# Forgetting attention in a two-layer decoder step: query, sample and memory steps tied by order edges to places between the heads, and the samples' scores taken one PSUM bank at a time

## The chip, the cores and the metric

The program runs on one core of one Trainium2 chip, in one launch. The metric is the device time of one execution in microseconds (us), lower is better. The engines are named as in the profile: PE (TensorE, matrix products), PEld (its weight loads), DVE (VectorE), ACT (ScalarE), POOL (GpSimd) and SP (SyncE, whose queue issues most of the DMA transfers). PE writes only to PSUM, whose eight banks of 128 x 512 float32 hold all products until DVE or ACT has read them.

## What is computed

One inference step of a trunk of two layers for a prompt of 512 tokens and eight samples of four new tokens each, width 1024. Layer 0 has a state-space and a sliding-window branch; layer 1, which the change touches, has forgetting attention. Every layer then has cross-attention into 256 memory tokens and a SwiGLU feed-forward part.

```python
def fox_attend(q, k, v, cum, q_off):
    '''Queries sit at key indices q_off..q_off+Tq-1; logit[t,s] += cum[t]-cum[s].'''
    ...
    bias = cq[..., :, None] - c[..., None, :]
    mask = jnp.arange(tk)[None, :] <= (q_off + jnp.arange(tq))[:, None]
    return gqa_attend(q, k, v, mask=mask, bias=bias)

def mem_kv(mem, g, wk, wv):
    b, m, _ = mem.shape
    mn = rms_norm(mem, g)
    return ((mn @ wk).reshape(b, m, XA_HEADS, XA_HEAD_DIM),
            (mn @ wv).reshape(b, m, XA_HEADS, XA_HEAD_DIM))
```

There are 16 query heads and 4 key heads of width 64. The prompt attends to itself in blocks of 128 queries; each sample attends to 1024 cached tokens, which lie in eight pages named by a table, and to its own four.

## The kernel before

All matrix products that need float32 precision are split: a weight piece of 128 x 1024 is loaded into one of two raw buffers (`wpiece`, L158), its high part made by ACT (L162) and its low part by DVE (L163) in one of three pairs of buffers, and three matmuls take the place of one (`acc3`, L138). The next load waits on SP's queue until a raw buffer has been split.

The attention of layer 1 is written in `odd`. Its prompt part has 64 **heads**: for each half m of the query heads (2), each block c of 128 queries (4) and each of eight query heads, `fox_prompt` computes scores (two matmuls of width W = 128(c+1) into a bank), then DVE subtracts the mask, negates and takes the row minimum (L1160, tensor_tensor_reduce), ACT takes the exponential with its sum (L1161), DVE the reciprocal (L1162), and POOL scales (L1163). Two heads later (`FOX_AHEAD`) the probabilities are transposed by PE (`tr`, L141), copied to `PT` by DVE or ACT (L1143), and after the eighth head of a block multiplied with the values (`pv`) and copied out (L1150). Heads 1 to 16 have W = 128 and 256, heads 17 to 32 have W = 384 and 512, heads 33 to 64 repeat this.

Between the heads three generators are advanced by a table of head numbers, `FOX_PLAN`:
- **q**: the second half of the query projection, eight steps of 24 matmuls (`linear_steps`), evacuated by DVE (L456);
- **s**: the samples, four groups G of two samples, in `fox_sample`: scores of 1024 cached tokens into two banks of the tag `sc` (a forget term from `S`, then the keys `fox_k`), scores of the new tokens (`sn`), maximum and exponential (L1272 to L1279), transposes (copied by ACT, L1288), the product with the values `fox_v`, its scaling into `sO` (ACT, L1296) and a transposition into q. The keys and values of group G + 1 are loaded through SP (L1237), 16 transfers each;
- **m**: the memory tokens' normalised operands (`mem_begin`: eight splits on ACT, L251, and on DVE, L252), then their keys and values (four steps of 24 and four of 12 wide matmuls).

After the heads the outcome is split (`oh`, `ol`) and multiplied with the output weights `wo_d`; the first products need only the first 256 tokens.

The order on each engine isn't the order in which the program is written. The program's order gives priorities; a scheduler that plays the program through with modelled times puts on each engine what is ready, and the result is the fixed order of that engine's queue. An order edge (`after`) holds one instruction behind another one in that order, without a semaphore. PSUM tiles are drawn by tag, and a tag's number of buffers caps how many of it live at once: `bufs = {"tr": 3, "sc": 2, "tp": 2, "pv": 1}`. Heads below 33 draw their score bank from `sc` alone, later heads from `['sc', 'sc', 'tr']` in turn.

Of the kernel before, what the change touches and what calls it, by code (L numbers as in the profile page):

```python
# [14 lines left out]
AF = mybir.ActivationFunctionType  # L15
ALU = mybir.AluOpType
# [3 lines left out]
P = 128  # L20
# [86 lines left out]
class Net:  # L107
    def __init__(self, nc, tc, ctx, I, O):
        self.nc, self.tc, self.ctx, self.I, self.O = nc, tc, ctx, I, O
        self.n = self.turn = 0  # L110
        self.hold = self.whold = self.last = None
# [25 lines left out]
    def mm(self, out, lhsT, rhs, start, stop):  # L137
        self.nc.tensor.matmul(out, lhsT, rhs, start=start, stop=stop)  # L138

    def tr(self, out, in_, k=P):  # L140
        self.nc.tensor.transpose(out, in_, self.ident[0:k, 0:k])  # L141
# [846 lines left out]
    def odd(self, st, nxt, fill):  # L988
        nc, tc, I, O = self.nc, self.tc, self.I, self.O
        with ExitStack() as es:  # L990
# [53 lines left out]
            with tc.tile_pool(name="fox", bufs=1) as fx:  # L1044
# [13 lines left out]
                self.banks = ['sc']  # L1058
# [4 lines left out]
                for m in range(2):  # L1063
                    for c in range(4):
# [22 lines left out]
    def fox_keys(self, kT, ncum):  # L1087
# [21 lines left out]
        self.zero(mask[:, 0:384])  # L1109
        self.after(nc.gpsimd.tensor_copy(mask[:, 384:512], self.cst[:, C_SWA + 128:C_SWA + 256]), self.last)  # L1110
# [15 lines left out]
    def fox_prompt(self, q, K2, V, m, c, ahead):  # L1126
# [4 lines left out]
        Q = self.fox_queries(q, m, tok)  # L1131
# [19 lines left out]
        for r in range(2):  # L1151
            for i in range(4):
                sc = self.bank([P, 512])
                for z in range(2):
                    self.mm(sc[:, 0:W], Q[z][:, r, i], K2[z][:, m, r, 0:W], z == 0, z == 1)
# [64 lines left out]
    def fox_sample(self, q, kTs, Qb, ncs, V, lf, fx, S, sel):  # L1220
# [25 lines left out]
        self.sample_q(q, Qb)  # L1246
        for G in range(4):
            sc = [self.psum("sc", [P, 4, 128]), self.psum("sc", [P, 4, 128])]
            sn = self.psum("tp", [P, 32])
            for u in range(2):  # L1250
                self.mm(sc[u].rearrange("p a b -> p (a b)"), sel[:, 128 * (G % 2):128 * (G % 2) + 128], S[:, G // 2, 512 * u:512 * u + 512], True, False)
                for b2 in range(2):
                    for m in range(2):
                        a = 64 * b2 + 32 * m
                        lq = Qb[:, 2 * G + b2, m].rearrange("p r i t -> p (r i t)")
                        self.mm(sc[u][a:a + 32], lq, keys[G, b2][:, 4 * u:4 * u + 4, 128 * m:128 * m + 128], False, True)
# [7 lines left out]
            wk = self.prt[:, 2560:4736]  # L1264
            pr = wk[:, 0:1056]
            gate = nc.vector.tensor_tensor(pr[:, 1024:1056], sn, c[:, C_MN + 32 * G:C_MN + 32 * G + 32], ALU.add)
            if G < 3:
                load(keys, G + 1, "fox_k")
            yield
            mx, nm, den, d1, rec = self.ty(3), self.ty(1), self.ty(3), self.ty(1), self.ty(1)  # L1270
            for u in range(2):
                nc.vector.tensor_reduce(mx[:, u:u + 1], sc[u].rearrange("p a b -> p (a b)"), AX.X, ALU.max)  # L1272
            nc.vector.tensor_reduce(mx[:, 2:3], pr[:, 1024:1056], AX.X, ALU.max)
            nc.vector.tensor_reduce(nm, mx, AX.X, ALU.max, negate=True)
            for u in range(2):
# [21 lines left out]
            self.sample_o(q, Osb, G, 1)  # L1297
            if G < 3:
                load(vals, G + 1, "fox_v")
            yield  # L1300


    def mem_begin(self, l):
# [12 lines left out]
        for k in range(KD):  # L1316
            g = self.par[:, G_MEM + 8 * l + k:G_MEM + 8 * l + k + 1]
            self.split(mh, ml, raw[:, k], k, 0, 256, g)
            if first:
                self.square_acc(acc, raw[:, k], k, 256)  # L1320
        if first:
            self.rstd(acc, self.mcol, self.mb, [(0, 0, 128), (1, 128, 128)])
# [381 lines left out]
    def run(self):  # L1704
# [5 lines left out]
        def memory(l):  # L1710
# [3 lines left out]
            m = self.mem_begin(l)  # L1714
# [129 lines left out]
```

## Time and profile before

| what | value |
|---|---|
| median of 3 runs | 1694.12 us (1693.13 to 1695.23) |
| profiled execution | 1698.67 us, span 1696.9 us |
| busy share of the span | PE 97%, PEld 89%, DVE 70%, ACT 46%, POOL 19% |
| chain that ended last | PE 91%, DVE 3%, POOL 2%, ACT 1%, DMA 1% |
| the heads of layer 1 | about 1005 to 1189 us of the span |

An engine's busy time counts its instructions from start to end. Matmuls are pipelined, so a busy PE need not be at its peak. An idle time is put down to the instruction whose semaphore ended it.

### The profile page before, as it was taken

The page shows a single profiled execution, that of the slowest core. Times are in us where ns is not written, and L with a number is a line of the kernel's source. Part 1 is how long each engine was busy: PE and PEld are TensorE (multiplying, and loading weights), DVE is VectorE, ACT ScalarE, POOL GpSimd, SP SyncE. Part 2 cuts the span into 40 slices and gives each one's busy share as a digit, 9 for nine tenths or more (in the row PEclk, how much of TensorE's full clock was granted, in tenths as well). Part 3 has the DMA queues.
Part 4 walks back from the last instruction along what each step waited for, and adds up shares of the span by engine and source line. Part 5 has one row for each costly group of instructions (what it writes and reads, how often), then busy time and mean ns, then how long its engine had stood idle before and what let it go on. Part 6 is the DMA issues. An engine that isn't in the chain of part 4 may idle for free.

```text
span 1696.9 us, 32362 instructions
## 1 busy us (share of the span) xinstructions
PE 1645.9 (97%) x12720; PEld 1518.7 (89%) x12720; DVE 1184.0 (70%) x2296; ACT 778.3 (46%) x1603; POOL 328.3 (19%) x510
## 2 busy tenths in 40 slices
PE   6999999998999999999999998998999999999997
PEld 6988899886997999999999996655988999999997
DVE  7667678867766887677766567654567877777663
ACT  5255445344444544444445355544545444444444
POOL 5022312657422310000001203111223100000002
PEclk9999999999999999999999999999999999999999
DMA  5211424126533233232323334554551233223222
GB/s 185 63 55 39 145 82 132 51 91 237 207 100 125 81 113 102 89 103 88 106 75 107 127 116 125 160 174 149 181 178 59 75 113 100 94 100 106 75 68 86
DMA packets 71221, 189.27 MB, mean 112 GB/s; under 512 B 7612, under 2 KB 34012, under 8 KB 63452
## 3 DMA queue, kind: packets, MB, share of 16 engines
q1 hardware_dynamic: 69388, 184.84, 32.9%
q8 instruction: 100, 1.64, 0.4%
q10 hardware_dynamic: 1600, 1.83, 0.4%
q0 software_dynamic: 80, 0.52, 0.1%
q14 instruction: 53, 0.43, 0.1%
HBM read 172.22 MB, written 14.95 MB: 110 GB/s over the span
## 4 chain that ended last, share of the span: by engine, by line
PE 91%; DVE 3%; POOL 2%; ACT 1%; issue 1%; DMA 1%; SPq 0%; DVEq 0%; POOLq 0%; ACTq 0%
PE ps L138 66%; PE ps L1563 22%; PE ps L141 3%; POOL room L425 1%; DMA room<-wo_d 0%; POOL sq L421 0%; DVE split_t L1544 0%; ACT prt L1161 0%; DVE prt L1160 0%; DVE xs L879 0%; ACT split_t L162 0%; DMA mem<-mem 0%; DVE meml L252 0%; DVE x L1730 0%; DMA x<-x 0%
## 5 line engine op out<-in xcount | busy, mean ns | idle before, releaser
L138 PE MATMUL ps<-xh,split_t 128*128 128x288 f32 (+1 forms) x2304 | 463.8, 294 | 13.8 <-ACT split_t L162 11.8
L138 PEld LDWEIGHTS ps<-xh,split_t 128*128 128x128 f32 x2304 | 371.1, 190 | 19.8 <-ACT split_t L162 12.8
L1563 PE MATMUL ps<-xf,split_t 128*128 128x272 f32 x2592 | 348.9, 289 | 3.1 <-DVE split_t L1544 2.1
L138 PE MATMUL ps<-xl,split_t 128*128 128x256 f32 (+1 forms) x1152 | 339.1, 295 | 1.2 <-DVE xl L252 1.0
L1563 PEld LDWEIGHTS ps<-xf,split_t 128*128 128x128 f32 x2592 | 335.0, 188 | 4.4 <-DVE split_t L1544 3.0
L261 POOL TENSOR_TENSOR room<-room,sq 128x256 f32<-128x256 f32 (+1 forms) x96 | 86.4, 904 | 773.4 <-ACT sq L260 771.7
L138 PEld LDWEIGHTS ps<-xl,split_t 128*128 128x128 f32 x1152 | 218.9, 190 | 6.9 <-issue 4.3
L138 PE MATMUL ps<-hh,fs 128*128 128x256 f32 (+1 forms) x1024 | 206.3, 288 | 0.0
L162 ACT CAST split_t<-room 128x1024 fp32r<-128x1024 f32 (+1 forms) x128 | 130.3, 1019 | 156.5 <-PE ps L138 112.3
L163 DVE TENSOR_TENSOR split_t<-room,split_t 128x1024 fp32r<-128x1024 f32 (+1 forms) x128 | 157.0, 1229 | 31.5 <-ACT split_t L162 31.0
L138 PEld LDWEIGHTS ps<-hh,fs 128*128 128x128 f32 x1024 | 164.9, 188 | 0.4 <-ACT fs L1607 0.4
L1544 DVE TENSOR_TENSOR split_t<-fr,split_t 128x1024 fp32r<-128x1024 f32 x108 | 131.7, 1221 | 35.3 <-ACT split_t L1543 35.0
L1543 ACT CAST split_t<-fr 128x1024 fp32r<-128x1024 f32 x108 | 113.4, 1052 | 89.6 <-PE ps L1563 53.4
L138 PE MATMUL ps<-hl,fs 128*128 128x256 f32 (+1 forms) x512 | 147.3, 288 | 0.0
L138 PE MATMUL ps<-oh,split_t 128*128 128x288 f32 (+1 forms) x512 | 105.7, 298 | 1.3 <-ACT oh L246 1.2
L138 PEld LDWEIGHTS ps<-hl,fs 128*128 128x128 f32 x512 | 96.4, 188 | 0.0
L138 PEld LDWEIGHTS ps<-oh,split_t 128*128 128x128 f32 x512 | 83.2, 192 | 8.3 <-issue 5.0
L138 PE MATMUL ps<-ol,split_t 128*128 128x288 f32 (+1 forms) x256 | 77.1, 301 | 0.3 <-DVE ol L249 0.2
L1607 ACT CAST fs<-room 128x512 fp32r<-128x512 f32 x64 | 39.4, 618 | 82.6 <-PE ps L138 68.3
L252 DVE SCALAR_TENSOR_TENSOR xl<-x,room,xh 128x256 fp32r<-128x256 f32 (+1 forms) x96 | 69.6, 755 | 5.6 <-ACT xh L251 5.6
L138 PE MATMUL ps<-hh,split_t 128*128 128x256 f32 (+1 forms) x384 | 73.4, 288 | 0.0
L1620 DVE TENSOR_TENSOR x<-x,ps 128x256 f32<-128x256 f32 (+1 forms) x128 | 54.4, 433 | 26.9 <-PE ps L138 26.7
(423 smaller groups left out, 3091.2 us busy)
## 6 DMA issues: line engine op xcount, KB each, us to landing
fr<-wfi SPq DMA_DIRECT2D x36, 1024.0 KB
room<-wfo SPq DMA_DIRECT2D x64, 256.0 KB
room<-wo_e SPq DMA_DIRECT2D x16, 512.0 KB
xk<-mem_k SPq DMA_DIRECT2D x8, 1024.0 KB
xv<-mem_v SPq DMA_DIRECT2D x8, 1024.0 KB
room<-wfi SPq DMA_DIRECT2D x16, 512.0 KB
fox_k<-fox_k SPq DMA_DIRECT2D x64, 128.0 KB
fox_v<-fox_v SPq DMA_DIRECT2D x64, 128.0 KB
```

What stands on the lines that cost most here:

```text
L138: self.nc.tensor.matmul(out, lhsT, rhs, start=start, stop=stop)
L141: self.nc.tensor.transpose(out, in_, self.ident[0:k, 0:k])
L162: nc.scalar.copy(hi[:, 0:n], raw[:, 0:n])
L163: nc.vector.tensor_tensor(lo[:, 0:n], raw[:, 0:n], hi[:, 0:n].bitcast(F32), ALU.subtract)
L252: return nc.vector.scalar_tensor_tensor(ll, src, g, hh.bitcast(F32), ALU.mult, ALU.subtract)
L261: nc.gpsimd.tensor_tensor(acc, acc, sq[:, 0:N], ALU.add)
L425: nc.gpsimd.tensor_tensor(acc, acc, sq, ALU.add)
L1543: nc.scalar.copy(hi, t)
L1544: nc.vector.tensor_tensor(lo, t, hi.bitcast(F32), ALU.subtract)
L1563: self.nc.tensor.matmul(ps, w[a][:, k], x[:, b, k], start=start and k == 0 and i == 0, stop=k == 3 and i == 2, skip_group_check=True)
L1607: nc.scalar.copy(hi, raw)
L1620: nc.vector.tensor_tensor(x, x, ps, ALU.add)
```

## The change

Five things change, all in layer 1's attention:
- the table `FOX_PLAN`, and a call `ready`, which builds the next block's queries four heads before the block begins;
- **order edges**: the first PE instruction of each generator step is held behind the score matmul of the head after which the step stands (`behind`, `placed`);
- **banks**: `tr` 4 and `sc` 3, and all heads draw from `['sc', 'sc', 'tr']`;
- **samples**: the scores come in two halves, each in one bank and a step of its own; DVE copies each half out with its row minimum (the fused operation of the heads, with zeros for the mask), so the bank is free before the exponential, which is then one ACT instruction over 1056 columns in place of three; the last transposition becomes a step of its own. A group has five steps in place of four, of which 17 stand in the table and the rest of the last group follows all heads;
- `mem_begin` is cut into four steps.

```diff
-for _a, _heads in (("q", range(4, 33, 4)), ("s", [33,34,36,38,40,41,43,45,47,49,51,53,55,57,59,61]), ("m", range(34, 64, 4))):
+for _a, _heads in (("q", (2, 4, 7, 10, 13, 16, 20, 24)), ("s", (25, 26, 28, 31, 33, 34, 36, 40, 41, 42, 44, 47, 49, 50, 52, 56, 58)), ("m", (19, 21, 23, 25, 35, 37, 39, 46, 54, 60))):
...
-        bufs = {"tr": 3, "sc": 2, "tp": 2, "pv": 1}[tag]
+        bufs = {"tr": 4, "sc": 3, "tp": 2, "pv": 1}[tag]
...
-        self.nc.tensor.matmul(out, lhsT, rhs, start=start, stop=stop)
+        return self.placed(self.nc.tensor.matmul(out, lhsT, rhs, start=start, stop=stop))
...
+    def placed(self, i):
+        if self.behind is not None:
+            self.behind, d = None, self.behind
+            self.after(i, d)
+        return i
...
-                self.banks = ['sc']
+                self.banks = ['sc', 'sc', 'tr']
...
-                        for _ in self.fox_prompt(q, K2, V, m, c, ahead):
-                            heads += 1
-                            self.banks = ['sc'] if heads < 33 else ['sc', 'sc', 'tr']
-                            for a in FOX_PLAN.get(heads, ""):
-                                next(gens[a], None)
-                self.fox_turn(ahead, 0)
+                blocks = [(m, c) for m in range(2) for c in range(4)]
+                ready = lambda m, c: self.fox_queries(q, m, slice(128 * c, 128 * c + 128))
+                Q = ready(*blocks[0])
+                for j, (m, c) in enumerate(blocks):
+                    for _ in self.fox_prompt(Q, q, K2, V, m, c, ahead):
+                        heads += 1
+                        if heads % 8 == 4 and j < 7:
+                            nq = ready(*blocks[j + 1])
+                        for a in FOX_PLAN.get(heads, ""):
+                            self.behind = self.scored
+                            next(gens[a], None)
+                        self.behind = None
+                    Q = nq
+                for _ in range(FOX_AHEAD):
+                    next(gens["m"], None)
+                    self.fox_turn(ahead, len(ahead) - 1)
...
+                nc.vector.tensor_tensor_reduce(pr[:, 512 * u:512 * u + 512], sf, self.zeros.to_broadcast([P, 512]), -1.0, 1e30, ALU.add, ALU.min, mx[:, u:u + 1])
+                if u == 0:
+                    yield
...
-            for u in range(2):
-                nc.scalar.activation(pr[:, 512 * u:512 * u + 512], sc[u].rearrange("p a b -> p (a b)"), AF.Exp, bias=nm, accum_out=den[:, u:u + 1])
-            nc.scalar.activation(pr[:, 1024:1056], pr[:, 1024:1056], AF.Exp, bias=nm, accum_out=den[:, 2:3])
-            nc.vector.tensor_reduce(d1, den, AX.X, ALU.add)
-            nc.vector.reciprocal(rec, d1)
+            nc.vector.tensor_reduce(nm, mx, AX.X, ALU.min)
+            nc.scalar.activation(pr, pr, AF.Exp, bias=nm, scale=-1.0, accum_out=den)
+            nc.vector.reciprocal(rec, den)
...
+            elif k % 2:
+                yield
```

The table shows little of where instructions now stand. Outside the attention of layer 1 the order of every engine is the same. Three places inside it follow (rows of equal instructions are merged with their count; the number behind a name tells tiles apart).

On PE around heads 18 to 20 (W = 384), before: `kh` and `kl` rows are a head's two score matmuls, `room,prt` rows transposes, a `PT` row the values' product, and the first row is the last matmul of the eighth query step.

```order
L138 MATMUL ps_12024<-xh_10309,split_t 128x288
L141 MATMUL ps_11580<-room,prt 128x128 x2
L141 MATMUL ps_11594<-room,prt 128x128 x2
L141 MATMUL ps_11608<-room,prt 128x128 x2
L138 MATMUL ps_11692<-kh_10826,qst 128x384
L138 MATMUL ps_11692<-kl_10827,qst 128x384
L141 MATMUL ps_11622<-room,prt 128x128 x2
```

The same place in the change:

```order
L138 MATMUL ps_11713<-kh_10826,qst 128x384
L138 MATMUL ps_11713<-kl_10827,qst 128x384
L138 MATMUL ps_11727<-kh_10826,qst 128x384
L138 MATMUL ps_11727<-kl_10827,qst 128x384
L141 MATMUL ps_11612<-room,prt 128x128 x2
L141 MATMUL ps_11655<-room,prt 128x128 x2
L138 MATMUL ps_11778<-kh_10826,qst 128x384
L138 MATMUL ps_11778<-kl_10827,qst 128x384
L138 MATMUL ps_11747<-kh_10826,qst 128x384
L138 MATMUL ps_11747<-kl_10827,qst 128x384
L138 MATMUL ps_11803<-xh_10099,split_t 128x256
L138 MATMUL ps_11803<-xl_10100,split_t 128x256
```

Before, all eight query steps are over by head 18. Now six stand before head 17, the seventh (`ps_11803`) behind head 20 and the eighth behind head 24; the scores of two heads stand together.

On ACT around the eight splits of the memory operands (`memh`), before; 128x512 and 128x128 rows of `prt` are exponentials of heads with that width:

```order
L1161 ACTIVATE prt,ty_12011<-prt,ty_12010 128x512
L1143 COPY PT_11901<-ps_12017 128x2x128
L1143 COPY PT_11902<-ps_12017 128x2x128
L1161 ACTIVATE prt,ty_12060<-prt,ty_12059 128x128
L251 ACTIVATE memh_12313<-mem_12308,room 128x256 x8
L1161 ACTIVATE prt,ty_12269<-prt,ty_12268 128x128
```

The same place in the change:

```order
L1176 ACTIVATE prt,ty_11889<-prt,ty_11888 128x384
L1158 COPY PT_11757<-ps_11895 128x2x128
L1158 COPY PT_11758<-ps_11895 128x128
L1137 CAST qst<-q_1101_11132 64x512
L1176 ACTIVATE prt,ty_11931<-prt,ty_11930 128x512
L258 ACTIVATE memh_11772<-mem_11767,room 128x256 x8
L1158 COPY PT_11757<-ps_11965 128x2x128
L1158 COPY PT_11758<-ps_11965 128x128
L1176 ACTIVATE prt,ty_11959<-prt,ty_11958 128x512
```

The splits move from behind head 33 to behind the first exponential of the heads 25 to 32; they are still eight in a row.

On SP where the output weights `wo_d` are loaded, before; `fox_v_13379` is the second half of the last group's values:

```order
L1237 DMA fox_v_13379<-fox_v 128x256
L1237 ISA
L1237 DMA fox_v_13379<-fox_v 128x256
L158 DMA room<-wo_d 128x1024 x2
L1351 DMA o_p_mem_v<-mkv_12306 128x1024
L1233 ISA x2
L158 DMA room<-wo_d 128x1024
```

The same place in the change, where two `wo_d` loads have gone out ahead of the first of the 16 value loads:

```order
L1252 DMA fox_v_13270<-fox_v 128x256
L165 DMA room<-wo_d 128x1024
L1252 ISA
L1252 DMA fox_v_13270<-fox_v 128x256
L1252 ISA
L1252 DMA fox_v_13270<-fox_v 128x256
L1252 ISA
L1252 DMA fox_v_13270<-fox_v 128x256
L165 DMA room<-wo_d 128x1024
L1368 DMA o_p_mem_v<-mkv_11765 128x1024
```

Before, two `wo_d` loads stand ahead of the last group's 16 key and 16 value loads and the third behind them all; now two stand between keys and values and the third ahead of the last three value loads. The last group's softmax, values' product and output stand among the first `wo_d` products on PE.

## Rows read from the trace of the kernel before

**Rows 1.** Stretches: busy time of each engine, PE clock, DMA share, GB/s

```profile
1005.00:1035.00 30.00, 30.00 (x232) 28.05 (x231) 23.98 (x78) 16.44 (x45) 6.14 (x14) 1.00 0.57 172
1035.00:1064.00 29.00, 24.22 (x120) 14.40 (x119) 21.89 (x71) 17.21 (x48) 10.43 (x21) 1.00 0.26 81
1064.00:1100.00 36.00, 34.85 (x307) 24.26 (x307) 25.30 (x84) 21.37 (x59) 6.05 (x13) 1.00 0.54 157
1100.00:1150.00 50.00, 48.09 (x348) 28.37 (x348) 26.71 (x94) 22.70 (x64) 8.30 (x16) 0.97 0.57 169
1150.00:1189.00 39.00, 33.14 (x246) 22.50 (x244) 18.47 (x57) 17.77 (x50) 5.36 (x8) 0.96 0.51 160
```

**Rows 2.** Waits in 1005 to 1035: us in total, times, longest

```profile
DVE ty L1162 <- ACT prt L1161: 3.2, 6, 0.7
```

**Rows 3.** Waits in 1035 to 1064

```profile
PEld ps L138 <- DVE ty L1160: 6.8, 9, 0.9
...
PE ps L138 <- DVE ty L1160: 3.5, 7, 0.7
DVE ty L1162 <- ACT prt L1161: 3.5, 6, 1.0
```

**Rows 4.** Timeline of DVE: start, duration, what, idle before and its releaser

```profile
1054.00 0.17 DVE L1162 RECIPROCAL ty<-ty 128x1 f32<-128x1 f32 x1 [0.98 <-ACT prt L1161]
1054.08 0.67 DVE L1160 CUSTOM_DVE_ANT_0 prt<-ps,prt 128x512 f32<-128x512 f32 x1
...
1055.73 0.67 DVE L1160 CUSTOM_DVE_ANT_0 prt<-ps,prt 128x512 f32<-128x512 f32 x1
```

**Rows 5.** Groups of DVE in 1003 to 1190: count, busy us, mean ns, idle before

```profile
L163 DVE TENSOR_TENSOR split_t<-room,split_t 128x1024 fp32r<-128x1024 f32 x13 | 16.0, 1234 | 5.3 <-ACT split_t L162 5.3
...
L1160 DVE CUSTOM_DVE_ANT_0 prt<-ps,prt 128x512 f32<-128x512 f32 x16 | 10.8, 673 | 0.0
...
L1272 DVE TENSOR_REDUCE ty<-ps 128x1 f32<-128x512 f32 x8 | 5.5, 689 | 2.8 <-PE ps L138 2.7
...
L252 DVE SCALAR_TENSOR_TENSOR meml<-mem,room,memh 128x256 fp32r<-128x256 f32 x8 | 3.4, 466 | 0.0
...
L456 DVE SCALAR_TENSOR_TENSOR q<-ps,room 128x288 f32<-128x288 f32 x5 | 2.3, 452 | 1.7 <-PE ps L138 1.6
```

**Rows 6.** Groups of ACT in 1003 to 1190

```profile
L1161 ACT ACTIVATE prt<-prt,ty 128x512 f32<-128x512 f32 x16 | 11.6, 724 | 7.4 <-DVE ty L1160 7.4
...
L1276 ACT ACTIVATE prt<-ps,ty 128x512 f32<-128x512 f32 x8 | 5.4, 683 | 5.7 <-DVE ty L1274 5.7
...
L251 ACT ACTIVATE memh<-mem,room 128x256 fp32r<-128x256 f32 x8 | 3.3, 496 | 0.0
```

**Rows 7.** Chain that ended last, 1000 to 1195: start, us, what

```profile
999.91 15.46 PE ps L138 x126
...
1066.22 1.50 PE ps L138 x9
...
1068.31 1.29 PE ps L138 x9
```

**Rows 8.** Timeline of SP

```profile
1074.76 8.99 SPq L1237 DMA_DIRECT2D fox_k<-fox_k  x16
...
1149.38 11.80 SPq L1237 DMA_DIRECT2D fox_v<-fox_v  x16
1161.29 0.85 SPq L158 DMA_DIRECT2D room<-wo_d  x2
```

**Rows 9.** Timeline of ACT

```profile
1167.35 1.04 ACT L162 CAST split_t<-room 128x1024 fp32r<-128x1024 f32 x1 [3.05 <-DMA room<-wo_d]
...
1169.53 0.38 ACT L1296 ACTIVATE sO<-ps,ty 128x128 f32<-128x128 f32 x1
```

**Rows 10.** Timeline of PE

```profile
1169.96 0.33 PE L141 MATMUL ps<-room,sO 128*128 128x128 f32 x1 [3.12 <-ACT sO L1296]
```

**Rows 11.** Stretches (columns as in rows 1)

```profile
1100.00:1104.00 4.00, 4.00 (x13) 2.00 (x14) 1.81 (x8) 1.50 (x6) 0.00 (x0) 0.57 0.86 227
...
1170.00:1175.00 5.00, 4.92 (x27) 4.72 (x28) 4.73 (x18) 2.98 (x8) 1.87 (x3) 0.67 0.38 108
```

**Rows 12.** Waits of PE in 1064 to 1189: us in total, times, longest

```profile
PE ps L138 <- DVE ty L1160: 1.2, 3, 0.6
PE ps L138 <- ACT prt L1276: 0.7, 1, 0.7
```

More of the change, by code (lines that the diff above doesn't have):

```diff
@@ L110, in __init__ @@
         self.n = self.turn = 0
-        self.hold = self.whold = self.last = None
+        self.hold = self.whold = self.last = self.behind = None
         pool = lambda name, **k: ctx.enter_context(tc.tile_pool(name=name, bufs=1, **k))
@@ L137, in mm @@
     def mm(self, out, lhsT, rhs, start, stop):
-        self.nc.tensor.matmul(out, lhsT, rhs, start=start, stop=stop)
+        return self.placed(self.nc.tensor.matmul(out, lhsT, rhs, start=start, stop=stop))
     def tr(self, out, in_, k=P):
-        self.nc.tensor.transpose(out, in_, self.ident[0:k, 0:k])
+        return self.placed(self.nc.tensor.transpose(out, in_, self.ident[0:k, 0:k]))
+    def placed(self, i):
[3 more added lines that the diff above has]
+        return i
     def wraw(self):
@@ L1124, in fox_queries, with fox_prompt @@
         return Q
-    def fox_prompt(self, q, K2, V, m, c, ahead):
+    def fox_prompt(self, Q, q, K2, V, m, c, ahead):
         nc = self.nc
@@ L1130, in fox_prompt @@
         tok = slice(128 * c, 128 * c + 128)
-        Q = self.fox_queries(q, m, tok)
         PT = []
@@ L1246, in fox_sample @@
         self.sample_q(q, Qb)
+        yield
         for G in range(4):
-            sc = [self.psum("sc", [P, 4, 128]), self.psum("sc", [P, 4, 128])]
             sn = self.psum("tp", [P, 32])
+            wk = self.prt[:, 2560:4736]
+            pr = wk[:, 0:1056]
+            mx = self.ty(3)
             for u in range(2):
-                self.mm(sc[u].rearrange("p a b -> p (a b)"), sel[:, 128 * (G % 2):128 * (G % 2) + 128], S[:, G // 2, 512 * u:512 * u + 512], True, False)
+                sc = self.bank([P, 4, 128])
+                sf = sc.rearrange("p a b -> p (a b)")
+                self.mm(sf, sel[:, 128 * (G % 2):128 * (G % 2) + 128], S[:, G // 2, 512 * u:512 * u + 512], True, False)
                 for b2 in range(2):
@@ L1255, in fox_sample @@
                         lq = Qb[:, 2 * G + b2, m].rearrange("p r i t -> p (r i t)")
-                        self.mm(sc[u][a:a + 32], lq, keys[G, b2][:, 4 * u:4 * u + 4, 128 * m:128 * m + 128], False, True)
+                        self.mm(sc[a:a + 32], lq, keys[G, b2][:, 4 * u:4 * u + 4, 128 * m:128 * m + 128], False, True)
+                nc.vector.tensor_tensor_reduce(pr[:, 512 * u:512 * u + 512], sf, self.zeros.to_broadcast([P, 512]), -1.0, 1e30, ALU.add, ALU.min, mx[:, u:u + 1])
+                if u == 0:
+                    yield
             for b2 in range(2):
@@ L1263, in fox_sample @@
                 self.mm(sn[a:a + 64], ncs.rearrange("p h t -> p (h t)"), self.ident[0:32, 0:32], False, True)
[L1264 to L1266 removed]
+            gate = nc.vector.tensor_tensor_reduce(pr[:, 1024:1056], sn, c[:, C_MN + 32 * G:C_MN + 32 * G + 32], -1.0, 1e30, ALU.add, ALU.min, mx[:, 2:3])
             if G < 3:
                 load(keys, G + 1, "fox_k")
[L1269 to L1279 removed]
+            nm, den, rec = self.ty(1), self.ty(1), self.ty(1)
+            nc.vector.tensor_reduce(nm, mx, AX.X, ALU.min)
+            nc.scalar.activation(pr, pr, AF.Exp, bias=nm, scale=-1.0, accum_out=den)
+            nc.vector.reciprocal(rec, den)
             yield
@@ L1300, in fox_sample @@
             yield
+            self.sample_o(q, Osb, G, 1)
     def mem_begin(self, l):
@@ L1320, in mem_begin @@
                 self.square_acc(acc, raw[:, k], k, 256)
+            elif k % 2:
+                yield
         if first:
@@ L1713, in memory @@
             nc.gpsimd.memset(t[:, 0:1], 0.0)
-            m = self.mem_begin(l)
+            m = yield from self.mem_begin(l)
             yield from self.mem_k(l, m, self.mk)
```

6 lines of the change are left out of this document (2 added, 4 removed).

## The prediction

> **What bounds the kernel now.** I read the stretches first [rows 1], since only the heads of layer 1 change: where does PE, the engine that the page puts at 97%, stand idle? In heads 1 to 16 (1005 to 1035) never: 30.00 of 30 us. In heads 17 to 32 (1035 to 1064) it is busy 24.22 of 29, in the next three stretches 34.85 of 36, 48.09 of 50 and 33.14 of 39. So 0 + 4.78 + 1.15 + 1.91 + 5.86 = 13.70 us of 184 are idle, and nothing that only fills PE can give more.
>
> Then the waits. In heads 17 to 32 PE and its weight loads wait for the row minimum that frees a score bank (L1160), 3.5 and 6.8 us in 16 pieces of up to 0.9 [rows 3]. The timeline of DVE shows why one bank more doesn't simply cure that [rows 4]: a head of width 512 takes DVE 1.65 us (1054.08 to 1055.73), of which 0.67 is the minimum and up to 0.98 is the reciprocal of an earlier head, standing in order ahead of the next minimum and waiting for its exponential. In this stretch DVE is busy 21.89 us and waits 3.5 for exponentials [rows 1, 3]; PE has no other work there, because all query steps are over and no sample or memory step has begun.
>
> Near the end one long wait is not of this kind. SP issues the last 16 value loads from 1149.38 for 11.80 us, and only then the `wo_d` loads, at 1161.29 [rows 8]. ACT waits 3.05 us for that weight with its split, at 1167.35, and what stands behind it, the scaling `sO`, begins at 1169.53 [rows 9]; PE waits 3.12 us for it at 1169.96 [rows 10]. From there the granted clock is 0.67 for 5 us, and once before, at 1100, 0.57 for 4 us [rows 11]: PE running at the lower of its two levels, 1.2 instead of 2.4 GHz, in part of each. Solving 0.5x + (L - x) = 0.57 x 4 and = 0.67 x 5 gives 3.4 us at half speed in both, so at most 1.7 us lost in each.
>
> **The parts of the change.** All are judged by stretches.
>
> *Heads 1 to 16.* Two of eight query steps leave. The chain of PE shows 126 matmuls in 15.46 us [rows 7], 0.123 us each, so 2 x 24 x 0.123 = 5.9 us leave and PE has 24.1 of 30. DVE has 23.98 busy and 3.2 of waiting for exponentials [rows 1, 2]; with two evacuations (0.45 each) and about one weight split (1.23) gone [rows 5], 25.1. So DVE paces the stretch: 25.1 if its waits don't grow, 30 if they take all that is offered. I take 28, as less PE work between the heads brings each exponential's wait nearer to the 1.65-us cycle of rows 4: **-2.0** (ends -4.9 and 0).
>
> *Heads 17 to 32.* PE gets the two steps (5.9) and, by the order, the first group's two score halves, 1.50 + 1.29 = 2.8 [rows 7]: 24.22 + 5.9 + 2.8 = 32.9. DVE gets eight memory splits (8 x 0.466 = 3.7), two evacuations (0.9), one weight split (1.2) and two halves of scores, 2 x 0.67 = 1.3 [rows 5]: 21.89 + 3.5 + 7.1 = 32.5. The bank waits go, their 3.5 us being covered by this work. Two engines with 32.9 and 32.5 don't overlap perfectly; I take 34 for 29: **+5.0**. Low end 32.9, +3.9. High end: ACT gets eight splits in a row, 8 x 0.496 = 4.0 [rows 6], behind the first exponential of heads 25 to 32; if they lie bare, 33 + 4 = 37, +8.
>
> *Heads 33 to 64 and after.* Gone: the first group's scores, -2.8, and the eight splits, which lay beside PE's work. The wait for `sO`, -3.1, with the half clock that follows it, -1.7: two `wo_d` loads now stand ahead of the last value loads, and the last group's `sO` is among the output products. The bank waits and the wait for a sample exponential, 1.2 + 0.7 [rows 12], -1.9: heads draw from three sorts of banks, and a sample bank is free after DVE's copy. The dip at 1100 may go with the moved steps, half of 1.7: -0.85. New: around heads 45 to 53 the order leaves PE mostly score pairs, transposes and one group's product, where DVE has heads of 1.65 to do and the halves' copies, where before ACT read the bank: 3 us, about two heads' cycles, **+3**. Sum -2.8 - 3.1 - 1.7 - 1.9 - 0.85 + 3 = **-7.4**. Lowest, if also the rest of the stretches' idle time goes: 1.15 + 1.91 + 5.86 idle, 3.4 of clock, 2.8 moved, -15.1. Highest, if the waits come back and the new one is twice as long: +3.
>
> *Edits that I count at nothing.* The samples' minima were DVE work already (0.689 each, rows 5), at 0.67 now. One exponential over 1056 columns takes the place of three, two of them 683 ns [rows 6]; ACT is busy 17.21 of 29 and 22.70 of 50 [rows 1], so it is covered; without that cover it costs about what the two cost, 1.4 us per group (an estimate from 2 x 0.683). The queries built four heads early are the same casts. On SP the next group's 16 keys, 8.99 us of issuing [rows 8], wait for the group before: in the order, first use stands two memory steps (5.9 us) and three heads behind, so at worst 1 or 2 us are bare, within the high end. The next weight load on SP waits behind those keys, but its step is ten heads on. `wo_d`'s earlier loads pass only the value loads, whose product comes after all heads.
>
> **Sum.** -2.0 + 5.0 - 7.4 = **-4.4 us**. Against the profiled execution, 1698.67, this gives 1694.3; that one lies 4.55 over the median of the runs, 1694.12, and the difference is taken from the median: **1689.7**.
>
> A second reading of room: weight loads are busy 28.05 of 30 us in heads 1 to 16, but 14.40 of 29 in heads 17 to 32 [rows 1], so PE's real room there may be more than 4.78 us. The Trainium skill (Perfetto Trace Analysis, section on identifying the most-contended engine) says that matmul busy time is a bad measure, as matmuls are pipelined, and weight-load busy share a better one; by that the moved 8.7 us would fit into the 29 us, and its total would be -9.4, towards the third rival; the sum above doesn't use it.
>
> **Rivals.**
> 1. *The late weight stays late.* The third `wo_d` load still stands behind 13 of 16 value loads, and its split on ACT ahead of late exponentials. For it: SP took 11.80 us for the 16. Against: the loads begin earlier, as the last group's gate comes earlier. Then the 3.1 and the 1.7 stay: -4.4 + 4.8 = +0.4, **1694.5**.
> 2. *Slower: ACT in front of DVE.* Where ACT does something long ahead of an exponential, DVE's reciprocal waits, behind it the next minimum, then PE for a bank, with nothing of its own left once the queries end at head 24. Heads 25 to 36 get the eight splits (4.0) and the first sample exponential (1.4); if these appear as waits and the 3.5 us of rows 3 double, the stretch is 33 + 5.4 + 3.5 = 42, +13 in place of +5; the same chain at heads 45 to 53 makes +3 into +6. Total -4.4 + 8 + 3 = +6.6, **1700.7**. It decides if PE waits over half a us per head there for L1160's successor. For it: rows 3 and 4 are this chain, and the splits stay eight in a row. Against: three score banks and a fourth for `tr` let PE run one or two heads ahead.
> 3. *All idle time fills.* 13.70 idle and 3.4 of clock are 17.1; if three quarters go, -13, **1681**. For: weight loads half idle. Against: DVE's 32.5.
> 4. *The clock.* Rows 1 show 1.00 in heads 17 to 32 in spite of gaps of up to 0.9. If the change made new stretches at half speed there, four of the 3.4-us kind would cost 6.8: +2.4, **1696.5**. The Trainium skill (TensorE: Matmul & The Clock Gate, section on PSUM-queue depth-cycling) says that frequent micro-idles between matmul groups make the gate oscillate; the trace doesn't show it there.
>
> **How the numbers follow.** About 0.2%, 3.4 us, is what a measurement of this kernel tells from no change. Forecast 0.38 (its spread of some 3 us puts 0.31 faster, 0.07 same), first rival 0.20 (0.03 faster, 0.15 same, 0.02 slower), second 0.22 (0.02 same, 0.20 slower), third 0.15 (faster), fourth 0.05 (0.02 same, 0.03 slower): faster 0.49, same 0.26, slower 0.25. The ends of all terms together reach from -16 (-4.9 + 3.9 - 15.1) to +11 (0 + 8 + 3), 1678 to 1705; leaving out the outer half of the second rival and a third of the third, some 0.16, gives 1680 to 1701. The forecast alone spans 1686 to 1693.
>
> **What would show it.** Right: no PE wait for L1160's successor in heads 17 to 32; that stretch, head 17's scores to head 33's, 33 to 35 us; heads 1 to 16 in 27 to 29, DVE's reciprocals waiting longer; no 3-us wait of PE for `sO`; one dip of the clock or none. Wrong: heads 1 to 16 still 30 us; heads 17 to 32 over 38 us with PE waiting for DVE; ACT's 3-us wait for `wo_d` still there with an exponential behind it; granted clock under 0.95 in heads 17 to 32.

## The result and the profile after

The change is slower: 1699.37 us median of 20 runs (1694.96 to 1701.96) against 1693.5 us; the ratio to before is 1.0033, 95% interval 1.0023 to 1.0043. Measured again (`c_again`), it was 1.0018 (1.0006 to 1.0031). One of the 20 runs of before, at 3568.73 us, is left out of the ratio as slow. The forecast was 4.4 us faster: the sign was wrong.

The profiled execution of the change took 1695.24 us (span 1693.4), less than its median and less than the 1698.67 of before. Single executions of one program differ by several us here, so one trace against one trace tells little. What helps is that PE's order differs only between two matmuls, one in the query projection (at 957.7 us in the change, 961.7 in before) and one in the output product (1212.5 and 1216.1). Between these marks, called **the attention** below, the three traced executions of each kernel compare like this (PE timelines, us from the first mark to the start of the 17th, 33rd, 49th and 64th score product and to the second mark; half clock is the sum of the stretches at 1.2 GHz in between):

| execution | 17th | 33rd | 49th | 64th | end | half clock |
|---|---|---|---|---|---|---|
| before, profile shown | 73.4 | 102.5 | 152.6 | 204.0 | 254.4 | 6.8 |
| before, b_1 | 73.4 | 102.5 | 151.2 | 202.6 | 252.1 | 3.4 |
| before, b_2 | 73.4 | 102.5 | 151.3 | 202.6 | 252.5 | 3.4 |
| change, profile shown | 72.0 | 102.5 | 153.9 | 205.5 | 254.8 | 10.2 |
| change, c_again | 72.0 | 102.5 | 153.8 | 205.4 | 254.6 | 10.2 |
| change, a_3 | 72.0 | 104.2 | 154.6 | 207.5 | 256.8 | 17.1 |

So the first 16 heads are 1.4 us shorter, the next 16 longer by as much, and the loss lies behind them: between the 33rd and the 49th score product the change takes 51.4 us (profile shown), where before took 48.7 to 50.1. The mean of the attention is 253.0 us before and 255.4 in the change; the mean half clock there is 4.5 us before and 12.5 in the change. At 1.2 GHz in place of 2.4, PE loses at most half of such a stretch, so the 8.0 us more can be up to 4.0 us of lost time, and the 2.4 us by which the attention grew can be half clock alone.

The scores show where PE is, and DVE can be further back. When head 33's scores are issued, DVE has taken 30 heads' minima in before and 27 in the change (in all three executions of each). Its 32nd minimum comes 105.4 us after the first mark in before and 112.3 in the change (first row before, second row the change); by the 36th it is level again, 120.0 and 118.9.

```profile
1067.13 0.67 DVE L1160 CUSTOM_DVE_ANT_0 prt<-ps,prt 128x512 f32<-128x512 f32 x1
1069.97 0.67 DVE L1175 CUSTOM_DVE_ANT_0 prt<-ps,prt 128x512 f32<-128x512 f32 x1
```

The stretches of the change that answer to [rows 1] (shifted by the 4 us; columns as there):

```profile
1001.00:1031.00 30.00, 27.77 (x207) 25.40 (x206) 23.52 (x78) 16.53 (x45) 6.13 (x14) 1.00 0.54 159
1031.00:1060.00 29.00, 27.16 (x152) 16.88 (x152) 23.16 (x74) 17.56 (x49) 9.62 (x18) 1.00 0.33 109
1060.00:1096.00 36.00, 32.68 (x280) 22.78 (x279) 21.55 (x81) 19.51 (x51) 6.82 (x13) 1.00 0.52 151
1096.00:1146.00 50.00, 46.00 (x344) 27.81 (x343) 21.81 (x81) 17.40 (x46) 6.58 (x13) 0.90 0.58 171
1146.00:1185.00 39.00, 35.26 (x269) 25.20 (x267) 23.59 (x74) 22.14 (x59) 7.93 (x12) 1.00 0.44 146
```

PE's idle time moved: 4.78 us in the second stretch became 1.84, but 1.15 and 1.91 in the third and fourth became 3.32 and 4.00 (the fifth's 5.86 became 3.74), and the fourth's clock fell from 0.97 to 0.90. The waits of PE over the attention of the change:

```profile
PE ps L138 <- DVE ty L1175: 6.1, 7, 2.3
PE ps L141 <- POOL prt L1178: 3.1, 1, 3.1
PE ps L138 <- ACT PT L1158: 2.1, 3, 1.2
```

The wait for `sO` of [rows 10] is gone. In its place stand one of 3.1 us for a scaled probability and, among those for a score bank (L1175 is the old L1160), one of 2.3 us. DVE's timeline shows what the first one waits for (start, duration, what, idle before):

```profile
1089.91 0.27 DVE L1175 CUSTOM_DVE_ANT_0 prt<-ps,prt 128x128 f32<-128x128 f32 x1
...
1090.42 0.42 DVE L1349 TENSOR_TENSOR mkv<-ps,room 128x256 f32<-128x256 f32 x1 [0.23 <-PE ps L138]
1091.45 0.29 DVE L1158 COPY PT<-ps 128x128 f32<-128x128 f32 x1 [0.61 <-PE ps L141]
1091.66 1.22 DVE L170 TENSOR_TENSOR split_t<-room,split_t 128x1024 fp32r<-128x1024 f32 x1
1092.91 0.42 DVE L1138 CAST qst<-qst 64x512 fp32r<-64x512 f32 x1
1093.35 0.69 DVE L1139 TENSOR_TENSOR qst<-q,qst 64x512 fp32r<-64x512 f32 x1
1094.07 0.16 DVE L1177 RECIPROCAL ty<-ty 128x1 f32<-128x1 f32 x1
```

Between a head's minimum at 1089.91 and the reciprocal at 1094.07 stand an evacuation of memory keys, a copy of probabilities, a weight split (1.22) and the next block's queries. On ACT the exponential between them stands behind the same weight's split and the same queries' cast:

```profile
1090.34 1.05 ACT L169 CAST split_t<-room 128x1024 fp32r<-128x1024 f32 x1
1091.42 0.62 ACT L1137 CAST qst<-q 64x512 fp32r<-64x512 f32 x1
1092.06 0.40 ACT L1176 ACTIVATE prt<-prt,ty 128x128 f32<-128x128 f32 x1
```

That exponential ends at about 1092.5 and the reciprocal comes at 1094.07, so some 1.5 us of the delay are DVE's own and the rest is ACT's. PE issued what it could until 1091.4 and then had no bank and no probabilities:

```profile
1091.38 0.28 PE L138 MATMUL ps<-kl,qst 128*128 128x256 f32 x1
1094.75 1.31 PE L141 MATMUL ps<-room,prt 128*128 128x128 f32 x9 [3.09 <-POOL prt L1178]
```

At 1117 PE waits for a bank, with the sample's exponential over 1056 columns (1178 ns each by ACT's groups) ahead of a head's minimum:

```profile
1117.01 0.16 DVE L1294 RECIPROCAL ty<-ty 128x1 f32<-128x1 f32 x1 [1.33 <-ACT prt L1293]
...
1117.09 0.40 DVE L1175 CUSTOM_DVE_ANT_0 prt<-ps,prt 128x256 f32<-128x256 f32 x1
...
1117.56 0.45 PE L138 MATMUL ps<-kh,qst 128*128 128x384 f32 x1 [2.27 <-DVE ty L1175]
```

The clock falls behind both; stretches of the change, answering to [rows 11]:

```profile
1090.00:1095.00 5.00, 1.91 (x16) 1.65 (x15) 3.52 (x11) 2.82 (x7) 0.75 (x2) 1.00 0.29 84
1095.00:1103.00 8.00, 7.81 (x90) 5.40 (x89) 4.01 (x20) 4.57 (x15) 2.67 (x6) 0.57 0.45 129
1103.00:1119.00 16.00, 12.73 (x81) 7.26 (x80) 7.34 (x24) 5.06 (x11) 0.48 (x1) 1.00 0.59 175
1119.00:1124.00 5.00, 4.46 (x23) 3.35 (x26) 2.57 (x13) 3.46 (x11) 1.50 (x4) 0.66 0.86 231
```

At 0.57 over 8 us and 0.66 over 5, PE ran at half speed for 6.8 and 3.4 us. On SP the rows that answer to [rows 8] are as the order promised. The third `wo_d` load goes out at 1149.80 in place of 1161.29, 7.5 us earlier once the 4 us between the two traces are taken off; the first two go out at 1140.91, where before had them at 1129.56:

```profile
1140.91 0.85 SPq L165 DMA_DIRECT2D room<-wo_d  x2
1142.01 7.68 SPq L1252 DMA_DIRECT2D fox_v<-fox_v  x13
1149.80 0.36 SPq L165 DMA_DIRECT2D room<-wo_d  x1
```

### The profile page after: what moved, and what is told of

Its sections match the earlier page's. It is cut to its first block, busy times and chain, and to the rows that moved or that the text cites. A ratio compares the mean times of both kernels' runs of the same rounds, so it can differ in the third digit from the quotient of the medians.

```text
span 1693.4 us, 32330 instructions
## 1 busy us (share of the span) xinstructions
PE 1639.8 (97%) x12720; PEld 1514.9 (89%) x12720; DVE 1183.7 (70%) x2300; ACT 776.5 (46%) x1587; POOL 329.1 (19%) x510
## 4 chain that ended last, share of the span: by engine, by line
PE 89%; DVE 5%; POOL 2%; ACT 2%; issue 1%; DMA 1%; DVEq 0%; POOLq 0%; ACTq 0%
PE ps L138 64%; PE ps L1580 22%; PE ps L141 3%; POOL room L432 1%; ACT memh L258 0%; ACT split_t L169 0%; POOL sq L428 0%; DVE split_t L1561 0%; DMA mem<-mem 0%; DVE xs L886 0%; DVE meml L259 0%; POOL col L303 0%; ACT prt L1176 0%; DMA room<-wo_e 0%; DVE x L1747 0%
## 5 line engine op out<-in xcount | busy, mean ns | idle before, releaser
L138 PE MATMUL ps<-hh,split_t 128*128 128x256 f32 (+1 forms) x384 | 73.4, 288 | 0.0
```

The lines of the kernel that those rows point to most:

```text
L138: return self.placed(self.nc.tensor.matmul(out, lhsT, rhs, start=start, stop=stop))
```

## Experiments

**Each kernel again.** `c_again` and `a_3` are the change, `b_1` and `b_2` the kernel before, unedited, for more executions.

> The changed kernel once more, for a second execution to look at. Theory A (waits): the attention of layer 1 gained at its end but lost about 9 us in new waits of PE in heads 38 to 60, and these stand in every execution at the same places; 1699 us (+5 to +6 over before), with half-clock stretches of no more than the 10.2 us of the first execution in there. Theory B (clock): those waits alone come out even, and the 5.6 us are half-clock stretches that most executions have and the first profiled one lacked; then this one shows 15 us or more of half clock in the attention, at places where PE has waited, or layer 0 differs.

> The change a third time. The two executions seen have half clock at the same places of the attention (6.8 us behind the 3.1-us wait for POOL at head 41, 3.4 us behind the 2.3-us wait for a bank at head 51). If these belong to the kernel: 711 to 712 from the attention's start to the end and the same places. If executions differ in there: other places, or 714 to 716.

> The kernel before once more, for a second execution to look at. From the start of layer 1's attention to the end its first profiled execution took 711.4 us, the change's two 711.8 and 711.5. If the two kernels really are even there: 711 to 712 again. If the first execution of before had more half-clock stretches there (6.8 us) than most have: 706 to 709, no half clock or one stretch in there, and the change is slower by what its own stretches and waits cost.

> The kernel before a third time. From the attention's start to the end its two executions took 711.4 us (6.8 us at half clock, at 1100 and 1172) and 709.0 (3.4 us, behind the wait for sO alone). If the stretch at 1100 is chance and the one behind sO belongs to the kernel: 709 to 711.5, half clock behind sO again. If the half clock of before is all chance: 707 to 709, none.

`c_again` gave 1.0018 (1.0006 to 1.0031). Both waits and the half clock behind them stand at the same places in all three executions of the change, so they belong to it. `a_3` has two more, at 1058 and 1160 (3.4 us each at half clock); its stretches there:

```profile
1056.00:1062.00 6.00, 4.90 (x12) 1.49 (x13) 4.06 (x12) 2.74 (x8) 0.69 (x1) 0.72 0.00 0
...
1160.00:1164.00 4.00, 3.31 (x10) 1.49 (x12) 2.78 (x12) 3.55 (x12) 1.66 (x3) 0.57 0.13 49
```

In before the one behind the wait for `sO` is there each time, the one at 1100 only once. The stretches of `b_1` there, with 0.72 over 6 us (3.4 at half clock):

```profile
1160.00:1165.00 5.00, 3.94 (x78) 3.00 (x74) 1.69 (x6) 2.50 (x5) 1.38 (x2) 1.00 0.91 291
1165.00:1171.00 6.00, 4.76 (x25) 4.57 (x26) 5.88 (x20) 4.08 (x13) 1.78 (x3) 0.72 0.35 102
```

Each run also records its mean granted clock. Over the 102 runs of before that have it on record it averages 0.9919 at 1694.4 us, over 33 of the change 0.9892 at 1698.6. At one and the same clock, 0.991, before took 1695.6 (27 runs) and the change 1697.0 (8 runs). At 0.990 and 0.992, with 3 runs of the change each, the difference is 2.5 and 0.1. So of 4.2 us some 0 to 2.5 is the schedule at equal clock, about 1.4 where there are most runs, and the rest goes with a lower clock. A mean clock lower by 0.0027 over 1696 us is 9.2 us more at half speed, and the table's attention has 8.0 more: most of the lower clock lies there. The attention of the traced executions shows 2.4 of the 4.2 us; where the other 1.8 lie isn't in any trace.

**Single parts undone.** `u_edges` drops the edges, `u_mem` moves the memory steps back, `u_exp` takes the samples' maxima and exponentials from the banks again:

```diff
-                            self.behind = self.scored
```

```diff
-("m", (19, 21, 23, 25, 35, 37, 39, 46, 54, 60))
+("m", (33, 33, 33, 33, 36, 40, 44, 48, 52, 56, 60))
```

```diff
-                nc.vector.tensor_tensor_reduce(pr[:, 512 * u:512 * u + 512], sf, ...)
+                nc.vector.tensor_reduce(mx[:, u:u + 1], sf, AX.X, ALU.max)
...
-            nc.scalar.activation(pr, pr, AF.Exp, bias=nm, scale=-1.0, accum_out=den)
+            for u in range(2):
+                nc.scalar.activation(pr[:, 512 * u:512 * u + 512], sfs[u], AF.Exp, bias=nm, accum_out=den[:, u:u + 1])
```

> The change without its order edges (same table, banks and samples). If the edges hold work behind waiting heads and so make the new waits: 3 to 6 us less than the change, 1693 to 1696. If the table and not the edges empties heads 38 to 60: within 2 us of the change, about 1699.

> The change with the memory steps back near their old places: the splits at head 33, the eight matmul steps at heads 36 to 60 by fours plus the rest. Theory A: heads 38 to 60 get PE work back, the waits there fall by 4 to 8 us, but heads 25 to 36 lose cover (3 us): 1693 to 1697. If the memory steps are not the cause: 1699 or more.

> The change with the samples' maxima and three exponentials read from the banks as before (still in two steps). If the one long exponential and the reciprocal that waits for it (4.7 us in 4 pieces on DVE, directly ahead of heads' minima) make the waits: 2 to 4 us less than the change, 1695 to 1697. If the banks held longer cost more: 2 us or more above the change, 1701 or more.

Ratios to before: 1.0036 (1.0024 to 1.0048), 1.0039 (1.0024 to 1.0054) and 1.0056 (1.0039 to 1.0073), on the chip of `c_again`. None gains; in the one traced execution of each, the attention took 261.1, 258.8 and 265.4 us. With the memory steps back (`u_mem`) the 33rd score product comes 2.1 us earlier than in the change, but the 49th 4.9 later. Without the edges the loss comes after the 64th (54.2 us from there to the end, 49.3 in the change). With banks held over two steps (`u_exp`) PE waits 2.4 us for one of the sample's exponentials and half clock rises to 23.9 us; the 33rd score product alone comes 7.1 us later. So undoing any one of these three parts doesn't take the loss away. What building the queries four heads early costs or gives was not run by itself, though their casts are part of what stands ahead of the reciprocal at 1094.07.

**The two places.** `e_rec` moves the sample's reciprocal one step later, `e_spread` puts the first four matmul steps of the memory at heads 36, 39, 42 and 47, and `e_wo` holds the splits of `wo_d` behind the last head's exponential and minimum (`soft`):

```diff
-            nc.vector.reciprocal(rec, den)
             yield
...
             yield
+            nc.vector.reciprocal(rec, den)
             pv = self.psum("pv", [P, 128])
```

```diff
-("m", (19, 21, 23, 25, 35, 37, 39, 46, 54, 60))
+("m", (19, 21, 23, 25, 36, 39, 42, 47, 54, 60))
```

```diff
+        if self.late is not None:
+            self.after(h, self.late[0])
+            self.after(d, self.late[1])
...
+                self.late = self.soft
```

> The change with the reciprocal of a sample group's sum one step later, ahead of the values' product, so that DVE doesn't wait for the 1056-column exponential directly ahead of a head's minimum. If that wait (4.7 us in 4 pieces) is what starves PE at heads 48 to 52: PE's 2.3-us wait for a bank goes and the half clock behind it, 2 to 4 us less than the change. If DVE then waits for the head's own exponential instead, which stands behind the long one on ACT: within 1 us of the change.

> The change with the first four memory steps of matmuls at heads 36, 39, 42 and 47 in place of 35, 37, 39 and 46, so that one fills the place at head 41 where PE waits 3.1 us for POOL and the clock falls for 6.8 us. If PE waits there for want of work: that wait and its half clock go, 3 to 6 us less than the change, 1692 to 1696. If DVE's chain is what is late and everything behind it comes as late: within 2 us of the change.

> The change with the splits of the output weights on ACT and DVE held behind the last head's exponential and minimum. In the change three of these splits (3.7 us of DVE, as much on ACT) stand among heads 57 to 62, where PE loses 5 us, and before none did. If they are what is late there: those 5 us shrink to 2 or less, but PE waits for the weight at the end by up to what ACT and DVE need for the first pieces (2 to 3 us); together 0 to 3 us less than the change. If the heads there wait for their own exponentials: no gain there and the wait at the end comes on top, 2 to 4 us more than the change.

1.0023 (1.0008 to 1.0038), 1.0052 (1.0034 to 1.0070), 1.0031 (1.0020 to 1.0041). In `e_rec` the wait at 1117 is gone, and one of 4.07 us stands before the 42nd score product instead. DVE's timeline has the same weight split and queries ahead of a reciprocal, and the split itself waits 1.61 us for ACT's half of it, which stands behind the long exponential:

```profile
1095.66 1.23 DVE L170 TENSOR_TENSOR split_t<-room,split_t 128x1024 fp32r<-128x1024 f32 x1 [1.61 <-ACT split_t L169]
1096.90 0.42 DVE L1138 CAST qst<-qst 64x512 fp32r<-64x512 f32 x1
1097.34 0.69 DVE L1139 TENSOR_TENSOR qst<-q,qst 64x512 fp32r<-64x512 f32 x1
1098.05 0.17 DVE L1177 RECIPROCAL ty<-ty 128x1 f32<-128x1 f32 x1
```

So the wait moved, as its second theory had it, and the time stayed that of the change. `e_spread` made the stretch from the 33rd to the 49th score product 58.6 us where the change has 51.4: so a lack of PE work alone doesn't explain the wait. `e_wo` brought the 64th score product 5.1 us earlier (200.4), and the end took back most of it: 253.3 against 254.8, with 6.8 us of half clock; its runs are no faster than the change. In the trace, what the three splits cost among the heads came back behind them.

**Samples and memory where before had them.** `d_sm` with the edges, `d_sm_ne` without; queries as in the change:

```diff
+("s", (32, 33, 33, 34, 36, 38, 40, 40, 41, 43, 45, 47, 47, 49, 51, 53, 55, 55, 57, 59, 61))
+("m", (34, 34, 34, 34, 38, 42, 46, 50, 54, 58, 62))
```

> The change with the samples' and memory's steps at the heads where before had them (samples from head 32 on, memory from 34), query steps as in the change. If moving them ahead of head 34 is what leaves heads 38 to 60 without PE work: the waits of 3.1 and 2.3 us and their half clock go, heads 25 to 32 lose their cover, 1693 to 1697. If heads 38 to 60 wait because DVE and ACT carry more there than PE: waits stay at other heads, 1698 or more.

> As d_sm, but without order edges: of the change only the banks, the new sample steps and the early query steps are left. If banks and samples alone gain (the waits for L1160's bank, 4.8 us in before): 1689 to 1693. If the scheduler, free to take what it thinks is ready, puts the waits elsewhere as it did in u_edges: 1697 to 1703.

1.0048 (1.0033 to 1.0062) and 1.0082 (1.0068 to 1.0095). With less among them heads 17 to 32 are faster (the 33rd score product at 99.4 and 99.0), but heads 33 to 48 take 62.6 and 60.9 us. With these samples and banks, before's places are worse than the change's.

**Idle work in the two waits.** `f_fill` repeats two heads' score matmuls into the same bank:

```diff
-                for z in range(2):
-                    self.scored = self.mm(sc[:, 0:W], Q[z][:, r, i], ..., z == 0, z == 1)
+                self.hc = getattr(self, "hc", 0) + 1
+                for z in range(2 + 2 * {43: 10, 51: 5}.get(self.hc, 0)):
+                    self.scored = self.mm(sc[:, 0:W], Q[z % 2][:, r, i], ..., z % 2 == 0, z % 2 == 1)
```

> The change with idle work on PE at its two longest waits: the two score matmuls of head 43 are issued ten times more and those of head 51 five times more, into the same bank with the same result (30 matmuls, about 4.2 us of PE by the 0.12 and 0.18 us between such matmuls). If the half clock follows PE's standing idle: the 6.8 us near 1096 and the 3.4 us near 1120 go, the mean granted clock rises by 0.002 to 0.003 and the time falls by 2 to 4 us under the change although PE has more to do. If the clock has another cause: half clock at the same places, time as the change or up to 2 us more.

1.0052 (1.0038 to 1.0067), 1702.51 us, some 4 us over the change for about 4.2 us of added matmuls. The longest wait of PE in 1086 to 1130 is 1.2 us now, and the half clock in the attention is 10.2 us as in the change, but later (3.4 us at 1102 and 6.8 at 1122). The first theory isn't borne out; since all work behind shifted too, what starts the half clock stays open. What the run does show is who sets the pace at the first place: with 20 matmuls more, DVE's minima of heads 34 to 42 come within 0.1 us of where the change has them, counted from the first mark, and the 49th score product comes 0.4 us later (154.3 for 153.9). There PE's idle time was room, and PE waited for the others. The loss lies behind: the 64th score product comes 4.5 us later (210.0) and the end 5.5 (260.3).

**The forecast's parts by themselves, on the kernel before.** `x_so` holds the split of the third and later `wo_d` pieces on ACT behind the last `sO`; `x_q` takes the change's head numbers for the queries and holds the last two steps behind heads 20 and 24; `x_soq` is both.

```diff
-        nc.scalar.copy(hi[:, 0:n], raw[:, 0:n])
+        h = nc.scalar.copy(hi[:, 0:n], raw[:, 0:n])
+        if self.so is not None:
+            self.wn += 1
+            if self.wn > 2:
+                self.after(h, self.so)
```

```diff
+                                self.behind = self.scored if a == "q" and heads >= 20 else None
                                 next(gens[a], None)
```

> The kernel before with one order edge on ACT alone: from the third output weight on, its split stands behind the last group's scaling sO, so that sO doesn't wait with it for the DMA. If the end of the attention is a gain of its own (the 2.2 to 3.1-us wait of PE for sO and the 3.4 us of half clock behind it, in all three executions of before): 3 to 4 us faster than before, 1690 to 1692, half clock near 1170 gone. If PE then waits for the late weight itself: within 1 us of before.

> The kernel before with the first terms of the forecast alone: the seventh and eighth query step held by order edges behind heads 20 and 24, nothing else of the change. If filling PE's idle time in heads 17 to 32 pays by itself (4.8 us idle there before, 5.9 us of matmuls moved, heads 1 to 16 shorter by about 2 us): 2 to 4 us faster than before. If heads 1 to 16 stay as long because DVE sets their pace, or heads 17 to 32 become as much longer as they are filled: within 1.5 us of before.

> The kernel before with both: the third output weight's split behind sO (3.5 us shorter in the attention in the execution seen) and the two query steps behind heads 20 and 24. If the two parts add up: 1686 to 1690. If the query steps are worth nothing: as x_so, 1691 to 1693.

> The kernel x_so once more, on the chip of the two others. Its attention took 248.9 us against 252.1 to 254.4 in before, but its median was only 1.1 us lower. If the difference in the attention is real and the rest chance: 2 to 3.5 us faster than before. If other parts take it back: about 1 us again.

| kernel | median, us | ratio to before (95%) | attention, us | half clock there |
|---|---|---|---|---|
| x_so | 1692.74 | 0.9993 (0.9983 to 1.0002) | 248.9 | 0 |
| x_so_2 | 1692.92 | 0.9989 (0.9979 to 1.0000) | 248.9 | 0 |
| x_q | 1692.77 | 0.9990 (0.9980 to 1.0000) | 248.9 | 0 |
| x_soq | 1690.87 | 0.9981 (0.9969 to 0.9992) | 249.0 | 3.4 |

In `x_so`, ACT scales first, and the split follows (its timeline, and the stretch that answers to the one of `b_1` at 1165):

```profile
1164.14 0.38 ACT L1301 ACTIVATE sO<-ps,ty 128x128 f32<-128x128 f32 x1
1164.40 2.00 ACT L163 CAST split_t<-room 128x1024 fp32r<-128x1024 f32 x2
```

```profile
1165.00:1171.00 6.00, 5.21 (x39) 4.55 (x39) 5.88 (x16) 4.79 (x12) 0.74 (x2) 1.00 0.40 128
```

The clock is 1.00 where `b_1` had 0.72. The attention is 3.2 us or more shorter in both executions, but the medians only 1.1 and 0.8 us, less than both expectations had for a gain of its own, and neither interval excludes no change. The runs of `x_so` have the same mean clock as the runs of before beside them (0.9924), so the half clock that its trace lacks is on average not missing from its runs; where they have it isn't in any trace. `x_soq` beats both kernels, and its interval excludes no change; it is the version to keep. That its two parts add up isn't shown: 1690.87 lies just above the 1686 to 1690 expected for that, its traced attention is no shorter than theirs, and the intervals overlap.

In `x_q` the two stretches are (columns as in rows 1):

```profile
1004.00:1034.00 30.00, 28.04 (x198) 24.00 (x196) 24.11 (x81) 15.92 (x47) 6.74 (x16) 1.00 0.59 176
1034.00:1063.00 29.00, 27.18 (x154) 17.88 (x155) 23.12 (x76) 17.91 (x49) 11.35 (x22) 1.00 0.30 91
```

From the attention's start to the 17th score product it takes 71.2 us (before 73.4), from there to the 33rd 29.5 (29.1). Two steps cost 0.4 us where they went and gave 2.2 where they had been. Its wait for `sO` is gone as well, without an edge for it, and that is most of its gain: against `b_1` it is 1.8 us ahead at the 33rd score product, 0.5 at the 64th and 3.2 at the end.

## Why the prediction was wrong

- *Heads 1 to 16, -2.0*: right in size. It was -1.4 in the change, -2.2 in `x_q`. For DVE as what paces them speaks that PE, now idle for 2.2 of 30 us, waits there for a minimum (1.2) and for queries (1.1), both DVE's. The reciprocals wait longer, as the forecast had it, in `x_q` (4.3 us for 3.2), but not in the change (3.0).
- *Heads 17 to 32, +5.0*: oversized by 3.6; it was +1.4. The step that failed is "Two engines with 32.9 and 32.5 don't overlap perfectly": PE's 32.9 was its busy time, 24.22, plus the moved matmuls at the 0.123 us of [rows 7]. But a matmul counts as busy from start to end, 0.28 us in the row at 1091.38 above, more than twice that. In `x_q` the 5.9 us raised the busy time only by 2.5 over `b_1`'s 24.64, to 27.18: a busy PE still had room. DVE's 32.5 didn't set the length either. The work came, and from the 16th to the 32nd minimum DVE takes 37.7 us in the change for 28.5 in before, but PE issued head 33's scores five minima ahead of it instead of two. The page on reading traces that was named there (the Trainium skill, Perfetto Trace Analysis, the section on the most-contended engine) would judge the room by weight loads, and the trace agrees: they were busy 14.40 of 29 us in before, and most of the work fitted.
- *Heads 33 to 64 and after, -7.4*: this term fell, and with it the sign. It came out at +0.4 against the profile shown of before and +2.7 against `b_1`. The half that went wrong is its **+3** for new waits. They were looked for at heads 45 to 53 as "about two heads' cycles"; in all three executions they are behind the 43rd score product (3.1 us), where none was looked for, and before the 52nd (2.3), where one was, and half clock, for which the term had put a gain of 1.7 and 0.85, came behind each of them, 10.2 us or more in place of 3.4 to 6.8. That is up to 3.4 us of lost time against `b_1`, as much as the whole +2.7. A head's cycle was priced by its own instructions; what DVE does between two heads, a weight split of 1.22 us and 1.1 of queries in a row, with 1.05 and 0.62 for the same on ACT, was counted as busy time spread over the stretch. This is read from the traces; that DVE and ACT set the pace there `f_fill` bears out, but no run takes the split or the queries away from the place, so which of them starts the wait stays open, as does what starts the half clock.
- *The wait for `sO`, -3.1 - 1.7*: right as a mechanism: `x_so` alone has neither, and an attention 3.2 us shorter than `b_1`. In the change the wait is gone too, but from the 49th score product to the end it takes 100.9 us like `b_1`: the wait before the 52nd score product, its half clock and the waits among the last heads, where the weight splits now stand, took it back.
- *Edits counted at nothing*: the exponential over 1056 columns wasn't covered. The step "ACT is busy 17.21 of 29 [...] so it is covered" looked at ACT's share, but the sample's reciprocal on DVE waits 1.3 us for it, directly ahead of a head's minimum. `e_rec` took that wait away and gained nothing, so its price is that of whichever item on DVE is late.
- *Rivals*: the first didn't come, as the wait for `sO` went. The second named the chain (ACT, reciprocal, minimum, bank) and gave 1700.7, close to the 1699.37 measured. That closeness is in the main luck: 8 of its 11 us over the forecast lay at heads 25 to 36, where PE had no such wait, and 3 at heads 45 to 53, where one came. The fourth had half clock as a loss, in heads 17 to 32; it came in heads 41 to 53. The clock stayed at 1.00 in heads 17 to 32 in two of the change's three executions.

## What to carry over

Where PE alternates with a chain of other engines, look for the longest run of other work that stands between two links of the chain on any engine, and price that; stage sums of busy time say that there is room and not whether it is reached. In the change, 2.9 us of PE's idle time went from heads 17 to 32 and 4.3 came in the two stretches behind; but putting the moved work back (`u_mem`, `d_sm`) made heads 33 to 48 longer still, so a lack of fill isn't the whole of it. And where single parts of a change can be made on the old kernel with a few order edges, make them there: the query steps' places and the edges behind `sO` gave 2.9 us (`x_soq`, 0.9981), where the whole rearrangement lost 3 to 6.

## What wasn't expected of the hardware

The same program's executions differ by their half-clock stretches: the recorded mean clocks of before go from 0.988 (one run, 1698.8 us) to 0.995 (three runs, 1690.8 us on average), about 1.1 us for each 0.001. One trace compared with one trace put the change 3.4 us ahead, 20 runs each put it 5.9 behind.
